# Regrouping the attention slots of a hybrid decoder trunk: scores and products with v in one group, nine projection matmuls on either side of the transposes

## The chip, the cores and the metric

The kernel runs on one core of a Trainium2 chip. Its time is the device time in microseconds of one execution. Three runs of the kernel before took 2824.10, 2826.37 and 2828.47 us; the median, 2826.37 us, is the time before.

The core has engines that run their own instruction lists side by side and meet at semaphores: TensorE (PE in the profile, with its weight loads listed apart as PEld), VectorE (DVE), ScalarE (ACT), GpSimd (POOL) and SyncE (SP), which only issues DMAs here. TensorE reads its operands from SBUF and writes to PSUM, which is used in eight banks of 128 x 512 float32.

## The reference

Two residual layers over 1024 tokens of width 1024, one sequence. Layer 0 mixes tokens by a chunked causal gMLP, layer 1 by causal dilated sliding-window attention; each is followed by a squared-ReLU MLP. Every sub-layer has the form

```python
h = x * (1.0 + scale) + shift            # from a conditioning vector
x = layer_norm(ALPHA * x + gate * f(h), g, b)
```

The change lies in the attention. It has 16 heads of 64 and three patterns, (window, dilation) = (128, 1), (512, 4), (2048, 16), each with its own q, k and v projection of `h` (a weight of 1024 x 9216 in all). For each pattern and head, blocks of 128 queries look at their own block of keys and the one before:

```python
s = einsum('bnqrhe,bnkrhe->bnrhqk', qb, kb) * (E ** -0.5) + bias   # ALiBi
s = where(valid, s, NEG)
m = max(s); p = exp(s - m); l = sum(p)
o = einsum('bnrhqk,bnkrhe->bnqrhe', p / l, vb)
lse = m + log(l)
```

The three patterns' outputs are then added with weights softmax(lse), and the sum is multiplied by an output weight.

## The kernel before, in words

All matmuls take float32 operands that are split into a high and a low part (`split`, L100 to L103: ScalarE casts the high part, VectorE subtracts for the low part), so that one product is three matmuls: high-high, high-low, low-high.

**Tiling of the attention.** Heads go in eight pairs. `order` lists the 24 combinations of pair and pattern, for each pair first dilation 16 (g = 2), then 4 (g = 1), then 1 (g = 0). PSUM's eight banks are shared out at the head of `attention`: two each for scores (`sc`), products with v (`pv`), projections (`mm`) and transposes (`tr`).

**The projections** are a generator, `project()`. A unit is q, k or v of one combination for one half of the tokens; it sums over eight blocks of 128 input features. One step of the generator is one block, three matmuls of 128 x 512 (L1134), and eight steps make a unit. After its last step the unit is taken out of PSUM: v by one ScalarE copy (L1141), q and k by two splits for the two heads (ScalarE and VectorE), q with an additional copy on GpSimd (L1150). When a unit of the second half begins, the weights of a later unit are loaded (SyncE) and split. Seven units are done ahead of the first slot, and from there the projections run ahead of the attention.

**The slots.** `slots` holds 8 x 24 + 8 slots, each with three positions. `attend` puts a combination's work into its eight slots, four for each head of the pair:

- position 0, `scores(m)` (L1191): four matmuls for two query tiles, in every slot; then on VectorE bias, scaling and minimum in one instruction a tile (L1214), and on ScalarE the exponential (L1216). `statistics` of the combination before also stands here, in its first slot.
- position 2, `transposes(m)` (L1236): two to four transposes of probability tiles into one `tr` bank, which ScalarE and VectorE split into `pThi` and `pTlo`. In a combination's first slot `values` (L1176) stands ahead of it, eight transposes of v. `transposes` stand in slots 0 to 3 of a head's four for dilation 4, in 1, 2, 3 and 3 for dilation 1, and in 1 and 3 for dilation 16 (`when`).
- position 1, one slot later, `weighted(m)` (L1249): the products of v with `pThi` and `pTlo`, and behind the last of a head the copy and addition of the two PSUM halves into `oT` (ScalarE L1279, VectorE L1280).

`merge` puts the combination of the three patterns' outputs into the first five slots of the next pair: reading the statistics back from DRAM, the weights (VectorE and ScalarE, L1319), writing and spreading them by DMA, three scalings of 128 x 1024 tiles (one on GpSimd, two on VectorE, L1347) and two additions (L1350). `affine_row` puts work on GpSimd and SyncE into position 1 of the first slots.

**The order.** The main loop (L1415) goes through the slots, and in each through the three positions; behind each position it takes two steps of `project()`, six matmuls:

```python
for pos in slot:
    for f in pos:
        f()
    for _ in range(2):
        if next(stream, True) and n >= last_group:
            ...
            next(fill, None)
```

From slot 183 on the projections are used up; from slot 184 on (`last_group`) the same places are filled with pieces of the output multiplication (`box["begin"]`, psd_wo in the profile), sixteen in all, whose loads are issued in `output()` at the first of them.

The order of this program is a priority, not the last word. A planner goes through it with its own costs and gives each engine its list: an instruction that it believes to be ready goes ahead of an earlier one that it believes is not. Each engine then works through its list strictly in order, and waits where an operand is late. Buffers are given out from pools of fixed size (two `tr` banks, two `pTlo` tiles and so on); an instruction that needs a buffer waits until the one who had it has been read.

Of the kernel before, what the change touches and what calls it, by code (L numbers as in the profile page):

```python
# [35 lines left out]
def trunk(ctx: ExitStack, tc: tile.TileContext, x, c, ada_w, ada_b, ln_g, ln_b, a_w_in, a_b_in,  # L36
# [1010 lines left out]
    def attention(before):  # L1047
# [6 lines left out]
        with ExitStack() as ph:  # L1054
# [345 lines left out]
            def output():  # L1400
                box["oT"] = [act_pair(f"oTs_{half}") for half in range(2)]
                res = Residual(2)
                for i in range(4):
                    res.acc[i] = qk.tile([P, D], F32, name=f"acc_2_{i}", tag=("q0", "q1", "k0", "k1")[i])
                out = box["out"] = OutRows(box["oT"], b_w_out[0], gate, res, prepare, "wo")
                for ch in range(2):
                    out.load(ch)
                    prepare(ch)
                box["begin"] = out.begin()
# [3 lines left out]
                next(stream)  # L1413
            fill = None
            for n, slot in enumerate(slots):  # L1415
                for pos in slot:
                    for f in pos:
                        f()
                    for _ in range(2):
                        if next(stream, True) and n >= last_group:  # L1420
                            if not box:
                                output()
                            fill = box["begin"]
                            next(fill, None)
# [5 lines left out]
    with ExitStack() as ph:  # L1430
        open_psum(ph, "A", tr=3, mm=5)
        done = mixer_a()
    done = mlp(1, done)
    out = attention(done)
    with ExitStack() as ph:
        open_psum(ph, "C", tr=3, mm=5)
# [29 lines left out]
```

## Time and profile before

| | |
|---|---|
| median of three runs | 2826.37 us |
| the profiled execution | 2823.26 us |
| its span, first to last instruction | 2821.5 us |
| mean granted TensorE clock | 0.992 |
| TensorE busy | 2742.5 us, 97% of the span |
| VectorE busy | 1943.7 us, 69% |
| ScalarE busy | 1411.1 us, 50% |
| first scores of the attention | at 1045.3 us |
| last projection matmul in a slot | at 2059.5 us |

A busy TensorE in this profile is one with a matmul under way. A matmul's duration reaches from its start to its modelled end and overlaps that of the next, so what a matmul takes from the engine's time is read from the distance between starts. A number in square brackets in a list by time is idle time of the engine before that instruction, with what ended it. A list of waits names who waited for whom, the total, the number of times and the longest.

### The profile page before, as it was taken

The numbers are of one execution on the slowest core, as the hardware profiler recorded it, in microseconds if no ns is written. First come the engines' busy times: TensorE is split into PE (matmuls) and PEld (weight loads), VectorE is DVE, ScalarE is ACT, GpSimd is POOL, SyncE is SP. The second block draws the span as 40 slices with busy tenths as digits, with TensorE's granted clock in tenths as the row PEclk, the third lists the DMA queues.
The fourth block names the chain that finished last, engine by engine and source line by source line (L and its number), as shares of the span: only waits on it lengthen the run. The fifth ranks groups of instructions, "written<-read, shape, count | busy, mean of one in ns | idle before, by whom it ended". The sixth has DMA issues, their size and how long they took to land.

```text
span 2821.5 us, 36888 instructions
## 1 busy us (share of the span) xinstructions
PE 2742.5 (97%) x13290; PEld 2277.4 (81%) x13290; DVE 1943.7 (69%) x3485; ACT 1411.1 (50%) x2613; POOL 213.9 (8%) x163
## 2 busy tenths in 40 slices
PE   6999999999999999999999999999999999999997
PEld 5777878887888878888888888888877788888886
DVE  6786798777877665556555555555659975577776
ACT  3334275555443455555555555555564755554331
POOL 1021000000000034101000000010201000000000
PEclk9999999999999999999999999999999999999999
DMA  7533347667846443212121212121215564485561
GB/s 254 171 106 112 120 139 232 205 220 256 317 155 194 141 150 106 62 46 61 39 69 39 69 31 69 39 69 39 84 51 175 172 211 151 150 306 190 176 214 58
DMA packets 300186, 384.15 MB, mean 136 GB/s; under 512 B 47532, under 2 KB 172884, under 8 KB 300004
## 3 DMA queue, kind: packets, MB, share of 16 engines
q1 hardware_dynamic: 300004, 381.80, 42.1%
q8 instruction: 104, 1.70, 0.3%
q14 instruction: 78, 0.64, 0.1%
HBM read 297.77 MB, written 83.97 MB: 135 GB/s over the span
## 4 chain that ended last, share of the span: by engine, by line
PE 76%; DVE 11%; DMA 7%; ACT 2%; issue 2%; POOL 1%; SPq 1%; DVEq 0%; POOLq 0%; ACTq 0%
PE psd L938 21%; PE psua L782 9%; PE psq L1134 8%; PE psv L1134 8%; PE psk L1134 7%; PE psuc L782 4%; DMA adaw<-in_ada_w_dram 3%; PE psd_wout L356 3%; PE pv L1262 2%; PE psub L782 2%; PE psu L356 2%; PE psd_wo L356 1%; PE sc L1208 1%; DVE adaacc L128 1%; PE pT L1239 1%
## 5 line engine op out<-in xcount | busy, mean ns | idle before, releaser
L782 PE MATMUL psua<-right,left 128*128 128x512 f32 x1536 | 363.6, 390 | 3.3 <-ACT right L102 1.7
L938 PE MATMUL psd<-rhi,lhi 128*128 128x512 f32 x896 | 350.1, 391 | 2.1 <-ACT part L813 2.1
L938 PE MATMUL psd<-rlo,lhi 128*128 128x512 f32 x896 | 349.6, 390 | 1.4 <-DVE rlo L103 1.3
L938 PE MATMUL psd<-rhi,llo 128*128 128x512 f32 x896 | 349.2, 390 | 0.0
L782 PEld LDWEIGHTS psua<-right,left 128*128 128x128 f32 x1536 | 287.1, 188 | 65.5 <-DVE right L103 3.1
L1216 ACT ACTIVATE p<-p,stat 128x128 f32<-128x128 f32 (+1 forms) x384 | 170.2, 444 | 230.9 <-DVE stat L1214 230.0
L1134 PE MATMUL psv<-hT,wv_hi 128*128 128x512 f32 x768 | 246.8, 403 | 2.4 <-DVE qlo L103 2.4
L1134 PE MATMUL psq<-hT,wq_hi 128*128 128x512 f32 x768 | 248.1, 404 | 0.0
L1134 PE MATMUL psk<-hT,wk_hi 128*128 128x512 f32 x768 | 247.3, 403 | 0.0
L103 DVE TENSOR_TENSOR pTlo<-pT,pThi 128x512 fp32r<-128x512 f32 (+1 forms) x160 | 98.0, 620 | 158.4 <-ACT pThi L102 157.5
L938 PEld LDWEIGHTS psd<-rhi,lhi 128*128 128x128 f32 x896 | 168.5, 188 | 38.3 <-ACT part L813 3.0
L938 PEld LDWEIGHTS psd<-rlo,lhi 128*128 128x128 f32 x896 | 168.6, 188 | 36.7 <-DVE rlo L103 2.4
L938 PEld LDWEIGHTS psd<-rhi,llo 128*128 128x128 f32 x896 | 168.5, 188 | 35.2
L782 PE MATMUL psuc<-right,left 128*128 128x512 f32 x768 | 187.7, 391 | 0.0
L128 DVE SCALAR_TENSOR_TENSOR adaacc<-adaw,silu_c,adaacc 128x512 f32<-128x512 f32 x168 | 130.9, 789 | 67.2 <-DMA adaw<-in_ada_w_dram 66.3
L782 PEld LDWEIGHTS psuc<-right,left 128*128 128x128 f32 x768 | 143.4, 188 | 30.0 <-DVE right L103 0.6
L1280 DVE TENSOR_TENSOR oT<-oT,pv 64x512 f32<-64x512 f32 x96 | 91.0, 948 | 109.5 <-ACT oT L1279 108.8
L1134 PEld LDWEIGHTS psv<-hT,wv_hi 128*128 128x128 f32 x768 | 133.8, 190 | 22.2 <-issue 2.8
L1134 PE MATMUL psq<-hT,wq_lo 128*128 128x512 f32 x384 | 151.4, 394 | 0.0
L1134 PE MATMUL psv<-hT,wv_lo 128*128 128x512 f32 x384 | 151.3, 394 | 0.0
L1134 PE MATMUL psk<-hT,wk_lo 128*128 128x512 f32 x384 | 150.6, 392 | 0.0
L1134 PEld LDWEIGHTS psk<-hT,wk_hi 128*128 128x128 f32 x768 | 133.7, 190 | 19.6
(250 smaller groups left out, 5842.3 us busy)
## 6 DMA issues: line engine op xcount, KB each, us to landing
lraw<-forms SPq DMA_DIRECT2D x112, 512.0 KB, 4.3
adaw<-in_ada_w_dram SPq DMA_DIRECT2D x192, 256.0 KB, 3.0
up<-in_mlp_w_up_dram SPq DMA_DIRECT2D x64, 512.0 KB, 3.8
forms<-s SPq DMA_DIRECT2D x128, 256.0 KB, 2.4
rraw<-in_mlp_w_down_dram SPq DMA_DIRECT2D x64, 512.0 KB, 4.5
forms<-part SPq DMA_DIRECT2D x96, 256.0 KB, 2.5
spill<-acc SPq DMA_DIRECT2D x24, 512.0 KB, 2.6
wq_raw<-in_b_w_qkv_dram SPq DMA_DIRECT2D x24, 512.0 KB, 3.7
```

The source lines that it names most:

```text
L103: return first, lo_engine.tensor_tensor(lo, src, hi, op=ALU.subtract)
L128: ins = V.scalar_tensor_tensor(acc[:], raw[:], silu_c[:, k : k + 1], acc[:], ALU.mult, ALU.add)
L356: T.matmul(dst, s[a], m[b], start=(n == 0), stop=(n == last))
L782: T.matmul(acc, w[:, a, k, :], right[p][:, b, k, :], start=p in (1, 2, 5) and k + a + b == 0, stop=k == 3 and a == 1, skip_group_check=True)
L938: T.matmul(sums[kind, m][:], l[a][:, k, m * P : (m + 1) * P], r[b][:, k, :], start=p in (1, 5, 2, 3) and kp + k + a + b == 0, stop=kp == K ...
L1134: T.matmul(p[:], wu[a][:, k * P : (k + 1) * P], hT[half][b][:, k, :], start=k + c_ == 0, stop=k == KD - 1 and c_ == 2)
L1208: T.matmul(scb[:, sl], my["qlo"][e][:, tq], keys[:, k0 : k0 + w], start=False, stop=True)
L1216: A.activation(pr[:, 0:w], pr[:, 0:w], AF.Exp, bias=nm, scale=-1.0, accum_out=l)
L1239: T.transpose(pst[:, o : o + P], probs[t][:, P : 2 * P] if has[t] else probs[t][:, 0:P], ident[:])
L1262: T.matmul(pvs[b][:, q0 % HALF : q0 % HALF + w_], stt, x_[:, o_ : o_ + w_], start=not begun[b], stop=left[b] == 0, skip_group_check=True)
L1280: V.tensor_tensor(dst, dst, sb, op=ALU.add)
```

## The change

The loop over a slot's three positions becomes a loop over two: positions 0 and 1 are run together, then position 2. Behind each of the two come three steps of the projections (or three pieces of the output multiplication) instead of two behind each of three. A slot still takes six steps.

```diff
             for n, slot in enumerate(slots):
-                for pos in slot:
+                for pos in (slot[0] + slot[1], slot[2]):
                     for f in pos:
                         f()
-                    for _ in range(2):
+                    for _ in range(3):
                         if next(stream, True) and n >= last_group:
                             if not box:
                                 output()
```

So a slot's program order on TensorE changes from scores, six projection matmuls, products with v, six, transposes, six to scores, products with v, nine, transposes, nine.

## The prediction

> **What bounds the kernel now.** I read the page's summary first, then the busy times of the attention stage, then who waits for whom on TensorE in that stage, then single slots in order of time.
>
> ```profile
> span 2821.5 us, 36888 instructions
> PE 2742.5 (97%) x13290; PEld 2277.4 (81%) x13290; DVE 1943.7 (69%) x3485; ACT 1411.1 (50%) x2613; POOL 213.9 (8%) x163
> ```
>
> The stage that the change touches, and what follows it until the last products with v (stretch, length, then busy time and instructions of TensorE, weight loads, VectorE, ScalarE, GpSimd; granted clock, DMA share, GB/s):
>
> ```profile
> 1045.30:2060.00 1014.70, 1011.64 (x5495) 858.87 (x5494) 574.69 (x1393) 557.93 (x1329) 137.54 (x114) 1.00 0.22 60
> 2060.00:2104.00 44.00, 40.94 (x224) 32.80 (x223) 29.21 (x71) 28.03 (x71) 5.20 (x3) 1.00 0.17 50
> ```
>
> TensorE is busy for 1011.64 of 1014.70 us at a granted clock of 1.00, VectorE and ScalarE for 57% and 55%. The stage ends when TensorE has worked off its list; the other engines matter only where a matmul meets an operand that is not ready. The largest of TensorE's waits there (total, times, longest):
>
> ```profile
> PE pT L1239 <- ACT p L1216: 2.3, 4, 1.0
> ```
>
> So 2.3 us in four places, a transpose (pT) waiting for its exponentials (p); the view has one smaller row of the same kind and none for a product with v (pv). One slot in order of time (start, duration):
>
> ```profile
> 1511.25 0.22 PE L1207 MATMUL sc<-k,q 128*128 128x128 f32 x1
> ...
> 1511.60 0.28 PE L1208 MATMUL sc<-k,qlo 128*128 128x256 f32 x1
> 1511.72 0.62 PE L1134 MATMUL psv<-hT,wv_hi 128*128 128x512 f32 x2
> 1512.18 0.40 PE L1134 MATMUL psv<-hT,wv_lo 128*128 128x512 f32 x1
> ...
> 1512.87 0.40 PE L1134 MATMUL psv<-hT,wv_lo 128*128 128x512 f32 x1
> 1513.11 0.28 PE L1262 MATMUL pv<-pThi,v 128*128 128x256 f32 x1
> ...
> 1513.40 0.27 PE L1262 MATMUL pv<-pTlo,v 128*128 128x128 f32 x1
> 1513.51 0.68 PE L1134 MATMUL psv<-hT,wv_hi 128*128 128x512 f32 x2
> ...
> 1514.96 0.27 PE L1239 MATMUL pT<-ident,p 128*128 128x128 f32 x1
> ...
> 1515.20 0.71 PE L1134 MATMUL psv<-hT,wv_hi 128*128 128x512 f32 x2
> ...
> 1516.67 0.22 PE L1207 MATMUL sc<-k,q 128*128 128x128 f32 x1
> ```
>
> Read starts, not durations, since matmuls overlap. Two projections take 1512.18 - 1511.72 = 0.46, so 0.23 each and six 1.38 us. The six take 1.39 behind the scores (1511.72 to 1513.11), 1.45 behind the products (1513.51 to 1514.96) and 1.47 behind the transposes (1515.20 to 1516.67). Scores take 0.47 (1511.25 to 1511.72), products 0.40, transposes 0.24. The slot is 5.42 us and has no hole.
>
> **The change, part by part.** No instruction is added or removed, no DMA either: a slot still has eighteen projections, and the projections last until the same slot. Only the order moves.
>
> *One hand-over less.* The projections behind the scores go; scores run straight into products. The hand-over that is lost is the one that cost 0.01 (1.39 against 1.38); the 0.07 behind the products and the 0.09 behind the transposes stay. Of 24 slots of a head pair 4 + 8 + 6 = 18 (dilations 16, 4, 1) have scores and products both. Seven pairs give 126, less the first slot, plus 10 in the last pair before the projections run out: 135. That is 135 x 0.01 = 1.4 us gained. Scores next to products stand nowhere in the trace while projections run, so this is bounded from the rows above: if what is saved is not the 0.01 but the mean of the three lead-ins, (0.01 + 0.07 + 0.09) / 3 = 0.057, the gain is 7.7 us; if the first product loses its cover and costs the 0.05 by which a 0.11 step (1513.40 to 1513.51) exceeds the 0.06 of a bare 128-column step (128 of a 512-column 0.23), the loss is 6.8 us. I take -1.4, the lead-in that really disappears.
>
> The Trainium skill (TensorE: Matmul & The Clock Gate, Part 3, The mechanism) states that a weight load overlaps running matmuls only when it targets another row group. All loads here are full height, so by that rule no cover exists to be lost or saved, this term would be 0 and the sum 1.4 us higher. The trace disagrees: the load of the first product starts within the projection of 1512.87, at
>
> ```profile
> 1512.88 0.19 PEld L1262 LDWEIGHTS pv<-pThi,v 128*128 128x128 f32 x1
> ```
>
> *Transposes come sooner after their scores.* Between them stood twelve projections and now stand nine: 3 x 0.23 = 0.69 us less for the chain scores, VectorE's minimum, ScalarE's exponential. Matmuls behind a waiting transpose wait too: the nine projections, then the next scores. Where the slack is thin is seen at dilation 16, in the slots where VectorE also scales the last pair's outputs. First the thin places' first and last (TensorE, then ScalarE):
>
> ```profile
> 1064.42 0.60 PE L1239 MATMUL pT<-ident,p 128*128 128x128 f32 x4
> ...
> 2009.77 0.71 PE L1239 MATMUL pT<-ident,p 128*128 128x128 f32 x2 [0.53 <-ACT p L1216]
> ```
> ```profile
> 1063.67 0.39 ACT L1216 ACTIVATE p<-p,stat 128x128 f32<-128x128 f32 x1
> ...
> 2009.62 0.39 ACT L1216 ACTIVATE p<-p,stat 128x128 f32<-128x128 f32 x1
> ```
>
> At 1064.42 the fourth transpose starts some 0.33 later, 0.69 after its exponential ended (1064.06); at 2009.77 it already waits. Of the 32 transpose groups of dilation 16 between these slots and around them, 17 have less than 0.69 us to spare over the closest hand-over that occurs. A typical one of slot 3 of a pair (start of scores and of transposes; exponential; the scaling that holds VectorE):
>
> ```profile
> 1594.89 0.22 PE L1207 MATMUL sc<-k,q 128*128 128x128 f32 x1
> 1598.08 0.62 PE L1239 MATMUL pT<-ident,p 128*128 128x128 f32 x4
> ```
> ```profile
> 1597.83 0.39 ACT L1216 ACTIVATE p<-p,stat 128x128 f32<-128x128 f32 x1
> ```
> ```profile
> 1595.05 1.23 DVE L1347 TENSOR_TENSOR oT<-oT,bc 128x1024 f32<-128x1024 f32 x1
> ```
>
> The exponential ends at 1598.22 and the fourth transpose starts just after; it cannot come 0.69 earlier. Adding up 0.69 less the present spare time over the 17 gives 8.3 us if all of it is exposed, 0 if the planner puts projections ahead. Transposes of dilations 1 and 4 I cost at nothing (a row of theirs stands below). I take half, 4.1 us, because these slots already show waits that the planner did not see: the 0.53 above is one of them.
>
> *Products come sooner after their transposes,* by 0.69 us, and by 2 x 0.69 = 1.38 where the split of the transposed probabilities is held by work that hangs on the slot's start (weight splits, projection evictions). Three places recur in each pair. The tightest, dilation 1, slot 2 (TensorE, ScalarE, VectorE):
>
> ```profile
> 1542.13 0.27 PE L1239 MATMUL pT<-ident,p 128*128 128x128 f32 x1
> ...
> 1543.96 0.28 PE L1207 MATMUL sc<-k,q 128*128 128x256 f32 x1
> ...
> 1545.82 0.29 PE L1262 MATMUL pv<-pThi,v 128*128 128x256 f32 x1
> ```
> ```profile
> 1540.62 0.49 ACT L1216 ACTIVATE p<-p,stat 128x256 f32<-128x256 f32 x1
> ...
> 1543.26 0.59 ACT L102 CAST pThi<-pT 128x512 fp32r<-128x512 f32 x1
> ```
> ```profile
> 1542.66 1.29 DVE L103 TENSOR_TENSOR wk_lo<-wk_raw,wk_hi 128x1024 fp32r<-128x1024 f32 x1 [0.27 <-ACT wk_hi L102]
> 1543.98 0.69 DVE L103 TENSOR_TENSOR qlo<-psq,q 64x512 fp32r<-64x512 f32 x1
> 1544.70 0.69 DVE L103 TENSOR_TENSOR pTlo<-pT,pThi 128x512 fp32r<-128x512 f32 x1
> ```
>
> The low half is ready at 1545.39, 0.43 before the product. VectorE goes through without a break from 1542.66, so it will not be ready sooner, while the product moves up by 1.38: 0.95 late. The transposes of 1542.13 show the cover of their kind: the exponentials that they need had ended by 1540.62, where ScalarE begins a later one, 1.5 us earlier; 0.8 of that is left, and if it went too each such slot would add its shortfall. The two others (product, then its low half):
>
> ```profile
> 1496.84 0.29 PE L1262 MATMUL pv<-pThi,v 128*128 128x256 f32 x1
> ...
> 1529.37 0.28 PE L1262 MATMUL pv<-pThi,v 128*128 128x256 f32 x1
> ```
> ```profile
> 1495.47 0.56 DVE L103 TENSOR_TENSOR pTlo<-pT,pThi 128x384 fp32r<-128x384 f32 x1 [0.56 <-ACT pThi L102]
> ...
> 1528.10 0.56 DVE L103 TENSOR_TENSOR pTlo<-pT,pThi 128x384 fp32r<-128x384 f32 x1
> ```
>
> Spare are 0.81 and 0.71, so late by up to 0.57 and 0.67. Over 7.5 pairs the three are 7.5 x (0.95 + 0.57 + 0.67) = 16.4 us at most, 0 at least. I take a quarter, 4.1 us, because on plain chains the planner has been right (first rival).
>
> *Behind the projections* (2060 to 2104 us) the same sixteen output pieces fill the same slots, three at a time instead of two. The window above has 44.00 - 40.94 = 3.1 us of idle TensorE; that is the bound either way, and I take 0. Weight loads, statistics and the merge's DMAs keep their slot; on SyncE's and GpSimd's queues those of the middle position pass two projection steps, 1.4 us, within slots of 5.4. I take 0, and what would uncover them is a merge whose scaling comes later, which is in the transposes' term.
>
> **Sum.** -1.4 + 4.1 + 4.1 = +6.8 us on the profiled execution's 2823.26, so 2830.1. That execution lies 3.1 us under the median of the runs, 2826.37 (2824.10 to 2828.47), so on their scale 2833.2. I call 0.2%, 5.65 us, about what a measurement can tell from no change; the sum lies just over it.
>
> **The rivals.** *The planner gives the time back (no change).* The order on TensorE is the planner's, which lets projections pass what it believes is not ready. It did so once a pair, where a transpose needs the bank that the transposes of v hold:
>
> ```profile
> 1492.37 1.03 PE L1182 MATMUL psvt<-ident,vT 128*128 128x128 f32 x8
> ...
> 1494.40 0.30 PE L1239 MATMUL pT<-ident,p 128*128 128x128 f32 x1
> ```
> ```profile
> L1239 PEld LDWEIGHTS pT<-ident,p 128*128 128x128 f32 x366 | 49.7, 140 | 16.1 <-ACT p L1216 5.8 <-DVE v L103 1.9
> ```
>
> The transpose stands directly behind those of v in the program, yet five projections came between, and no idle TensorE is recorded there. If it sees every late operand so well, the order before is restored in the thin places and both waiting terms fall to about 1 us each: 2826.4 - 1.4 + 2 = 2827. Against it: the waits of the table above, which it did not foresee. It decides below 5.65 + 1.4 = 7.1 us of exposed waiting. This includes that the change does not do what it says: where products are late, projections again part them from scores.
>
> *Fewer groups are worth more than the scores' lead-in (faster).* If every change of kind on TensorE costs the same and one of three goes, 135 x 0.057 = 7.7 us go with no wait in return: 2818.7. For it: lead-ins of 0.07 and 0.09 exist. Against it: the one that goes is 0.01. It decides once a join saves 5.65 / 135 = 0.042 us.
>
> **How the numbers follow.** Waits partly exposed, slower by over 0.2%: 0.47, the forecast, with a range of its own from 2832 to 2848. Its top is all of both waiting terms: 2826.4 - 1.4 + 8.3 + 16.4 = 2849.7, cut a little because the waits cannot all be missed. Planner restores: 0.36, 2821 to 2832. Faster: 0.17, 2814 to 2821. The range 2820 to 2848 leaves out most of the faster case and the tip of the slower.
>
> **What would show it.** Right: on TensorE in 1045 to 2060 us products (pv) appear as waiting for pTlo, which they do nowhere now, above all in slot 2 of dilation 1; transposes' 2.3 us grow to 5 to 8; the slot of 5.42 us without waits shrinks to 5.41; nine projections behind the transposes take 9 x 0.23 + 0.09 = 2.16. Wrong: no wait on pv and projections standing between scores and products (first rival), or plain slots of 5.38 us and less (second).

## The result, and the profile after

| | before | after |
|---|---|---|
| median of five runs each, side by side | 2826.37 us | 2845.51 us |
| lowest to highest | 2824.10 to 2830.36 | 2842.94 to 2847.96 |
| ratio | | 1.0063, 95% interval 1.0050 to 1.0077 |
| span of the profiled execution | 2821.5 us | 2841.6 us |

The changed kernel is 19.1 us slower by the medians; the ratio with its interval, taken over the runs side by side, is 1.0063. The forecast was 2833.2 us in a range of 2820 to 2848: the sign and the range held, and the loss was nearly three times the 6.8 us of the sum.

The page of after, its span and first part (engine, busy time, share, instructions):

```profile
span 2841.6 us, 36856 instructions
PE 2752.7 (97%) x13290; PEld 2277.9 (80%) x13290; DVE 1944.5 (68%) x3485; ACT 1413.9 (50%) x2613; POOL 220.1 (8%) x163
```

Each engine has as many instructions as before, in 20 us more. TensorE's busy time grew by 10.2 us, that of the others by at most 6.2. The attention stage of after and what follows it until the last products (stretch, length, busy time and instructions of TensorE, weight loads, VectorE, ScalarE, GpSimd; granted clock, DMA share, GB/s):

```profile
1045.30:2079.00 1033.70, 1021.16 (x5498) 857.97 (x5496) 577.02 (x1394) 560.96 (x1330) 138.53 (x114) 1.00 0.21 59
2079.00:2122.00 43.00, 40.18 (x222) 32.50 (x221) 28.53 (x70) 27.74 (x70) 5.58 (x3) 1.00 0.21 50
```

Nearly all of the loss lies in the stage, at the same granted clock of 1.00: idle TensorE grew from 3.1 us to 12.5. The stretch behind it is not longer. Who waits for whom on TensorE in that stage of after (total, times, longest):

```profile
PE pT L1239 <- DVE v L103: 3.6, 8, 0.5
PE pv L1262 <- DVE pTlo L103: 3.5, 9, 0.5
PE pT L1239 <- ACT p L1216: 2.4, 9, 0.6
PE pT L1242 <- ACT p L1216: 1.2, 6, 0.3
```

Together 10.7 us, where before had 3.1 in the same window. The growth is less than the stage lost. One reason is that an idle stretch is counted from the modelled end of the matmul before it. The Trainium skill (Perfetto Trace Analysis, Tensor Engine Instruction (MATMUL, LD_WEIGHTS)) says the same, that the profiler works a matmul's end out and does not observe it; the trace fits that (slot 8 below: 0.43 recorded where the slot grew by 0.61). So I read the loss from starts: from one slot's first scores matmul to the next one's. From the first slot's start to the end of slot 181 the stage takes 1010.75 us before and 1029.00 after. The difference by place in a pair's 24 slots (0 to 7 dilation 16, 8 to 15 dilation 4, 16 to 23 dilation 1), added up over the pairs, here and for the experiments that follow, in us against before:

```
slot of 24                           1     2     3     4     5     7     8     9    10    11    12    13    14    15    18  others   sum
after                              0.9   4.6   1.9  -0.2  -0.5   0.1   5.0  -0.1   3.0  -0.1  -0.5   1.5   1.7  -0.2   1.9    -1.0  18.3
1 copy behind exponentials         1.0   4.6   1.8  -0.3  -0.5   1.8   5.1  -0.1   0.1   1.2  -1.2   1.0  -0.1  -0.1   2.0    -1.1  15.3
2 v split first                    0.9   4.7   1.8  -0.2  -0.5   1.8  -0.1   5.7   2.9  -0.1  -1.2   0.9   1.5  -0.2   2.0    -1.1  18.8
3 k low half on GpSimd             0.5  -0.1   3.2   0.7  -0.5   0.1   5.0  -0.1   0.3  -0.1   5.2   0.7   1.6  -0.2   1.7    -0.8  17.3
4 only dilation 1                 -0.3   0.0  -0.4   0.0  -0.4   0.0   0.0   0.0   0.0   0.0   0.8   0.0   0.0   0.0   1.9    -0.6   0.9
5 scores 9, products+transposes 9  0.0   0.0  -2.1   0.0  15.5   1.9   6.4  -0.7  -0.7   5.0  -1.7  -0.7  -0.6  -0.2  -0.3     0.0  21.7
6 the same, 12 and 6              -0.1   0.0  -3.0  -0.1   7.8   0.7   5.7   0.2  -0.7  -0.7  -0.4  -0.7  -0.6  -0.6  -0.3    -1.7   5.3
7 the same, 15 and 3              -0.3   0.1  -3.3   0.1  27.9  -0.1  -3.5  11.8  -0.7  -0.7  -1.8  -0.7  -0.6  -0.6  -0.4     7.7  34.6
8 the change, 12 and 6            -0.3   4.9  -2.8   2.8  -0.9   0.8  -0.1   2.9  -0.1  -0.1  -1.1   1.3  -0.1   3.3   2.0     0.7  13.0
9 the change but seven slots      -0.1   0.0  -2.1   2.8  -0.1   0.1  -0.1   3.0  -0.1   1.2   1.0   0.0   0.0   3.3  -0.2    -1.1   7.7
10 = 6 from slot 9 on              0.0   0.0   0.2   0.0  -0.6   0.0   0.0  -0.6  -0.7  -0.7  -0.1  -0.7  -0.6  -0.6  -0.3    -1.3  -6.1
11 = 6 and v split first           0.2   0.0  -3.0  -0.1   7.5   0.9  -0.5  -0.6  -0.7  -0.7   1.3   0.1  -0.6  -0.6  -0.3    -1.7   0.9
```

Seven places of each pair (2, 3, 8, 10, 13, 14, 18) carry nearly all of the loss of after; most of the others gain a little. (The column of others hides two larger terms: slots 0 and 6 of row 7 with 3.1 and 6.9, and slot 23 of row 8 with 1.7.) The spans differ by 2 us more; that is mostly what follows the last products, 718.2 us before and 720.3 after, and since it lies between 717.5 and 721.1 over all the profiled runs here, I leave it as scatter.

A slot of dilation 4 without waits (TensorE of after, the same slot as the prediction's; start, duration):

```profile
1520.14 0.22 PE L1207 MATMUL sc<-k,q 128*128 128x128 f32 x1
...
1520.60 0.28 PE L1262 MATMUL pv<-pThi,v 128*128 128x256 f32 x1
...
1521.01 0.67 PE L1134 MATMUL psv<-hT,wv_hi 128*128 128x512 f32 x2
...
1523.13 0.27 PE L1239 MATMUL pT<-ident,p 128*128 128x128 f32 x1
...
1523.38 0.71 PE L1134 MATMUL psv<-hT,wv_hi 128*128 128x512 f32 x2
...
1525.54 0.22 PE L1207 MATMUL sc<-k,q 128*128 128x128 f32 x1
```

Scores 0.46, products 0.41, nine projections 2.12, transposes 0.25, nine projections 2.16: 5.40 where it was 5.42. So the new order itself costs nothing. Three lossy places show what does.

**Slots 10 and 14** (dilation 4, 3.0 and 1.7 us over the pairs). ScalarE in slot 10 of the fifth pair, before:

```profile
1634.51 0.40 ACT L1216 ACTIVATE p<-p,stat 128x128 f32<-128x128 f32 x1 [1.15 <-DVE stat L1214]
...
1634.91 0.49 ACT L1216 ACTIVATE p<-p,stat 128x256 f32<-128x256 f32 x1
...
1635.51 1.07 ACT L1279 COPY oT<-pv 64x512 f32<-64x512 f32 x1
```

And after, ScalarE, the end of the second scaling on VectorE, and TensorE:

```profile
1645.79 0.40 ACT L1216 ACTIVATE p<-p,stat 128x128 f32<-128x128 f32 x1 [1.15 <-DVE stat L1214]
...
1646.19 1.05 ACT L1279 COPY oT<-pv 64x512 f32<-64x512 f32 x1
1647.04 0.49 ACT L1216 ACTIVATE p<-p,stat 128x256 f32<-128x256 f32 x1
```
```profile
1645.96 0.08 DVE L1214 DVE_READ_ACCUMULATOR2_ANT stat<- 128x1 f32 x1
```
```profile
1647.26 0.27 PE L1239 MATMUL pT<-ident,p 128*128 128x128 f32 x1
1647.67 0.33 PE L1242 MATMUL pT<-ident,p 128*128 128x128 f32 x1
```

The products now end 1.4 us sooner in the slot, so the eviction copy of the head is ready sooner, and the planner gave it the place between the two exponentials. The second exponential starts 0.85 behind the copy instead of right behind the first, and the second transpose 0.41 behind the first instead of 0.11. The Trainium skill (PSUM — Partial Sum Buffer, Engine vs sequencer instructions) states that ScalarE's queue is strictly first in, first out; the trace agrees: the exponential's minimum had been read out on VectorE at 1646.04, and it started at 1647.04, behind the copy.

**Slot 2** (dilation 16, 4.6 us). VectorE and TensorE of after:

```profile
1597.37 1.23 DVE L103 TENSOR_TENSOR wk_lo<-wk_raw,wk_hi 128x1024 fp32r<-128x1024 f32 x1 [1.65 <-ACT wk_hi L102]
1598.51 0.68 DVE L103 TENSOR_TENSOR qlo<-psq,q 64x512 fp32r<-64x512 f32 x1
1599.11 0.67 DVE L103 TENSOR_TENSOR pTlo<-pT,pThi 128x512 fp32r<-128x512 f32 x1
```
```profile
1599.22 0.27 PE L1262 MATMUL pv<-pThi,v 128*128 128x128 f32 x1
1599.84 0.33 PE L1262 MATMUL pv<-pTlo,v 128*128 128x128 f32 x1 [0.35 <-DVE pTlo L103]
```

The low half ends at 1599.78 and the second product waits for it: 0.62 between the two starts instead of 0.06 or 0.07. The same place before had its low half at 1590.31, 1.0 us ahead of its use:

```profile
1589.64 0.67 DVE L103 TENSOR_TENSOR pTlo<-pT,pThi 128x512 fp32r<-128x512 f32 x1
```
```profile
1591.31 0.27 PE L1262 MATMUL pv<-pTlo,v 128*128 128x128 f32 x1
```

**Slot 8** (first slot of dilation 4, 5.0 us). VectorE of after splits v here behind the last addition of dilation 16's outputs, and the transposes need the bank that this split frees:

```profile
1635.69 1.08 DVE L1280 TENSOR_TENSOR oT<-oT,pv 64x512 f32<-64x512 f32 x1 [1.37 <-ACT oT L1279]
1636.80 1.29 DVE L103 TENSOR_TENSOR v<-psvt,v 128x512 fp32r<-128x512 f32 x2
```
```profile
1637.54 0.33 PE L1239 MATMUL pT<-ident,p 128*128 128x128 f32 x1 [0.43 <-DVE v L103]
```

They start 6.06 us after the slot's first scores (1631.48). Before it was 6.17 (1620.88 to 1627.05), but with seventeen projections ahead of them. Now there are fourteen, so the transposes could start 0.69 sooner; they start only 0.11 sooner, and the rest comes out as a wait.

### The profile page after: what moved, and what is told of

The parts are those of the page before. It is cut to its first block, busy times and chain, and to the rows that moved or that the text cites. A ratio compares the mean times of both kernels' runs of the same rounds, so it can differ in the third digit from the quotient of the medians.

```text
span 2841.6 us, 36856 instructions
## 1 busy us (share of the span) xinstructions
PE 2752.7 (97%) x13290; PEld 2277.9 (80%) x13290; DVE 1944.5 (68%) x3485; ACT 1413.9 (50%) x2613; POOL 220.1 (8%) x163
## 4 chain that ended last, share of the span: by engine, by line
PE 73%; DVE 11%; DMA 7%; ACT 5%; issue 2%; POOL 2%; SPq 0%; DVEq 0%; ACTq 0%; POOLq 0%
PE psd L938 21%; PE psua L782 10%; PE psv L1134 8%; PE psq L1134 7%; PE psk L1134 5%; PE psuc L782 5%; DMA adaw<-in_ada_w_dram 3%; PE psd_wout L356 3%; PE psub L782 2%; PE pv L1262 2%; PE psd_wo L356 2%; ACT p L1216 1%; DVE adaacc L128 1%; PE psu L356 1%; PE sc L1208 1%
## 5 line engine op out<-in xcount | busy, mean ns | idle before, releaser
L1214 DVE CUSTOM_DVE_ANT_0 p<-sc,bias 128x128 f32<-128x128 f32 (+1 forms) x384 | 119.7, 347 | 68.6 <-PE sc L1208 66.2
L1134 PEld LDWEIGHTS psq<-hT,wq_hi 128*128 128x128 f32 x768 | 135.7, 189 | 22.2
```

What stands on the lines that cost most here:

```text
L1134: T.matmul(p[:], wu[a][:, k * P : (k + 1) * P], hT[half][b][:, k, :], start=k + c_ == 0, stop=k == KD - 1 and c_ == 2)
L1214: V.tensor_tensor_reduce(out=pr[:, 0:w], in0=scb[:, sl], in1=st["bias"][:, width - w :], scale=-0.125, scalar=3e38, op0=ALU.add, op1=ALU.m ...
```

## The experiments

Theory A: the loss is operands that come too late at named places, because the order of ScalarE's and VectorE's lists no longer suits TensorE's. Theory B: scores and products side by side cost in themselves, 135 times a little. Each group of experiments ran beside the kernel before on the same chip; its medians there were 2826.53 (experiments 1 to 4), 2822.10 (5 to 8) and 2827.08 us (9 to 11). The expectations in microseconds count from 2826.5, so for 5 to 8 the ratios are compared. A ratio is taken over the runs and is not the quotient of two medians. All kernels compute the whole of the reference.

**1. The copy behind both exponentials.** The change, with the copy of dilation 4 (one per half of a head, issued where its products end) held in program order on ScalarE.

```diff
-                        if m < len(packs) - 1:
+                        if m < len(packs) - 1 and not (g == 1 and m == 1):
                             return
...
-                        for b in range(2):
+                        for b in range(2) if g != 1 else (m // 2,):
...
-                            A.copy(dst, sa)
+                            ins = A.copy(dst, sa)
+                            if g == 1:
+                                tc.keep_in_program_order(ins)
```

> The changed kernel with one difference: at dilation 4 the copy of the first PSUM half of the products (ScalarE, L1279 of the kernel before) is held behind the slot's second exponential instead of between its two. TensorE's and VectorE's lists stay as in the changed kernel; 16 pairs of ScalarE instructions swap. Theory A (the loss is late operands at named places): the transposes of slots 2 and 6 of dilation 4 no longer wait, which was 3.0 and 1.7 us over the stage against before, so 2845.5 - 4.7 = 2841, slots 106 and 110 back to about 5.41 us. Theory B (the loss is the price of scores and products standing together, 19.1 us over 135 joins): no change, 2845.5.

Measured 2840.9 us, ratio 1.0049 (1.0035 to 1.0062). This interval overlaps with that of the change, 1.0050 to 1.0077, so the time alone says little; the places do. The two exponentials of slot 10 stand together again (ScalarE):

```profile
1646.81 0.40 ACT L1216 ACTIVATE p<-p,stat 128x128 f32<-128x128 f32 x1 [1.15 <-DVE stat L1214]
...
1647.21 0.50 ACT L1216 ACTIVATE p<-p,stat 128x256 f32<-128x256 f32 x1
...
1647.70 1.06 ACT L1281 COPY oT<-pv 64x512 f32<-64x512 f32 x1
```

Slots 10 and 14 gave back all of their 4.7 us. Slot 11 now loses 1.2, and slot 7 of the first pair 1.7 once, so the stage is 2.9 us shorter than in the change, and that the time came out at the expected 2841 is partly chance. The cause of slots 10 and 14 is shown; experiment 3 adds a condition for slot 10.

**2. The split of v first.** The change, with the last copy and addition of dilation 16 issued behind the split of v and held there in program order.

```diff
+            held = []
...
                               pst[:].rearrange("p (t e c) -> p t e c", e=2, c=HEAD))
+                    if held:
+                        held.pop()()
...
+                            if g == 2 and e == 1 and b == 1:
+                                def evict(dst=dst, sa=sa, sb=sb):
+                                    tc.keep_in_program_order(A.copy(dst, sa))
+                                    tc.keep_in_program_order(V.tensor_tensor(dst, dst, sb, op=ALU.add))
+                                held.append(evict)
+                                continue
                             A.copy(dst, sa)
                             V.tensor_tensor(dst, dst, sb, op=ALU.add)
```

> The changed kernel with one difference: in the first slot of dilation 4 the copy and addition of the last products of dilation 16 go behind the split of the transposed v, on ScalarE and on VectorE; TensorE's list stays. Theory A: the transposes there wait for the bank that the split of v frees, and the split stands behind that copy and addition; they come 0.6 us sooner in each of eight pairs, so 2845.5 - 5 = 2840.5, slot 104 from 7.37 to about 6.75 us. Theory B: no change, 2845.5.

Measured 2844.45 us, 1.0064 (1.0051 to 1.0076), the time that theory B expected. By place it is not theory B. Slot 8 gave back its 5.0 us, as expected, and slot 9 took on 5.7. The products there now wait behind the addition; this row was 3.5, 9 in the change:

```profile
PE pv L1266 <- DVE pTlo L103: 6.8, 16, 0.5
```

The cause of the wait in slot 8 is shown, and the time was not gained: it was passed on to the next operand in VectorE's list.

**3. The low half of k's weights on GpSimd.** It takes the 1.23 us ahead of the low half in slot 2 away from VectorE.

```diff
-                    return unit(b_w_qkv[0, :, c0 : c0 + P], f"w{'qkv'[X]}_{hp}_{g}")
+                    return unit(b_w_qkv[0, :, c0 : c0 + P], f"w{'qkv'[X]}_{hp}_{g}", lo_engine=G if X == 1 else V)
```

> The changed kernel with the low half of the k weights made by GpSimd instead of VectorE (24 tiles of 1.23 us). Theory A: in slot 2 of dilation 16 and slot 2 of dilation 1 the products wait for the low half of the probabilities, which stands on VectorE behind that split; these two waits (4.6 and 2.0 us over the stage against before) go, so 2845.5 - 6.5 = 2839. Theory B: no change beyond 1 us.

Measured 2840.39 us, 1.0055 (1.0042 to 1.0068), by the time alone not clear of the change. Slot 2 gave back its 4.6 us. Slot 10 gave back 2.7 of its 3.0, which was not expected: its copy still stands between the two exponentials, but without the split of k's weights on VectorE the first of them starts 1.06 us after the slot's first scores instead of 1.52. So in slot 10 the place of the copy costs time only when the scaling is late as well. Slot 18 kept 1.7 of 1.9, a miss: the planner no longer parted its products with projections. Slot 3 lost 1.3 more, slot 4 0.9, and a single wait of 4.2 us stands in slot 12 of the first pair (ScalarE, then TensorE):

```profile
1120.54 1.04 ACT L102 CAST wv_hi<-wv_raw 128x1024 fp32r<-128x1024 f32 x1 [6.76 <-DMA wv_raw<-in_b_w_qkv_dram]
...
1121.96 0.40 ACT L1216 ACTIVATE p<-p,stat 128x128 f32<-128x128 f32 x1
```
```profile
1122.51 0.33 PE L1239 MATMUL pT<-ident,p 128*128 128x128 f32 x1 [4.23 <-ACT p L1216]
```

Here ScalarE stood idle for 6.76 us ahead of a cast of weights whose load had not landed, and the exponentials stood behind the cast. This slot of the first pair differs from run to run, from 5.3 to 8.4 us in the twelve other profiled runs, but here it takes 11.8. The load was issued 0.9 us after the slot's first scores; in the other runs it was 0.8 to 6.4 us ahead of them. In SyncE's list it stands directly behind the write of an affine row, which waits for GpSimd, and GpSimd now also makes k's low halves, 2.4 us each. So the edit is the likely cause; no run has isolated it.

**4. The change in the slots of dilation 1 alone,** 42 of the 135 hand-overs.

```diff
-                for pos in slot:
+                for pos, steps in (((slot[0] + slot[1], 3), (slot[2], 3)) if n // 8 % 3 == 2
+                                   else ((slot[0], 2), (slot[1], 2), (slot[2], 2))):
...
-                    for _ in range(2):
+                    for _ in range(steps):
```

The last line is the same in experiments 5 to 10, where it is left out; long lines are broken here.

> The kernel before with two groups of nine only in the slots of dilation 1 (42 of the 135 joins). Theory A: these slots account for 1.1 us of the changed kernel's loss, so 2826.4 + 1.1 = 2827.5. Theory B: 42 / 135 of 19.1 us, so 2826.4 + 5.9 = 2832.3.

Measured 2827.11 us, ratio 1.000 (0.999 to 1.001). The stage is 0.9 us longer: 1.9 in slot 18, 0.8 in slot 12, the rest gains. Theory A's 2827.5 fits; theory B's 2832.3, a ratio of 1.0021, lies outside the interval.

**5 to 7. Two groups divided elsewhere:** the scores alone, then products and transposes together, with 9 and 9, 12 and 6, or 15 and 3 projections behind them. One hand-over fewer per slot, as in the change, but scores and products stay apart. The edit of experiment 6 is shown; 5 has 3 and 3 in place of 4 and 2, and 7 has 5 and 1.

```diff
-                for pos in (slot[0] + slot[1], slot[2]):
+                for pos, steps in ((slot[0], 4), (slot[1] + slot[2], 2)):
```

> Two groups again, but divided elsewhere: the scores alone, nine projections, then the products with v and the transposes together, nine projections. Order of TensorE: scores 4, projections 9, products 4, transposes 3, projections 9. One join per slot fewer than before, exactly as in the change, and nine projections in a row, as in the change. The transposes stand 9 projections behind their scores (before 12), as in the change; the products stand 18 behind their transposes instead of 12 (in the change 9). Theory A (late operands: what the change lost came from products too close to their transposes, and from transposes too close to their scores): of the change's 18.2 us by place, slot 2 of dilation 16 (4.6) and slot 18 (2.0) are waits of the products and go; the copies on ScalarE between the two exponentials at slots 10 and 14 (4.7) came from the products ending later in the slot than before, and here they end later still, so these may stay; slot 3 (1.9) and slot 8 (5.0) are waits of transposes and may stay. So 2826.5 plus 5 to 12, about 2834, range 2826 to 2839. Theory B (scores and products with v in one group is what costs): gone, as they are parted: 2826.5, or a little below. Theory C (two groups of nine projections cost as such, whatever stands between them): the change's whole loss again, 2845.

> As the run with the scores alone and nine projections, but twelve projections behind the scores and six behind the products and transposes. Order of TensorE: scores 4, projections 12, products 4, transposes 3, projections 6. The transposes stand 12 projections behind their scores, as before; the products stand 18 behind their transposes (before 12). One join fewer than before, as in the change. Theory A (late operands at named places): no operand comes later than before, so no new wait but those that the later end of the products brings to the copies on ScalarE; 2826.5 less up to 3, that is 2824, range 2821 to 2832. Theory C (two groups cost as such): 2845. Theory of the join (each join that is saved is worth 0.057 us, 135 of them): 2826.5 less 7.7, 2818.8; with 0.01 for each, 2825.

> The scores alone, fifteen projections, products and transposes together, three projections. The transposes stand 15 projections behind their scores (before 12), the products 18 behind their transposes (before 12). Theory A: the transposes' waits that stand in the kernel before (2.3 us and 0.2 us recorded behind the exponentials) go as well, and one join per slot is saved: 2826.5 less 2.5 and less 1.4, about 2822.5, range 2816 to 2832; what can go against it is that three projections behind the transposes hide less of the evictions that free the banks of the next scores and products. Theory C: 2845.

Measured: 2844.44 us, 1.0074 (1.0062 to 1.0086), with 9 and 9; 2829.75, 1.0029 (1.0020 to 1.0039), with 12 and 6; 2861.66, 1.0138 (1.0125 to 1.0151), with 15 and 3. Theory C (two groups of nine cost as such) could live with the first but not with the second. Theory B's 2826.5 failed with 9 and 9, where scores and products stand apart and the loss is as large as the change's. The time that was expected from a join worth 0.057 us, 2818.8, failed too, though experiment 10 will show that these joins save about that much; the waits hid it. Theory A's numbers missed as well, by more than their ranges in all three, and in the last two a gain was expected and a loss came. Of the places it was right about slots 2 and 18, which are free of waits; slots 10 and 14, which it thought might stay, are free too (it had the direction wrong: in the change the products end sooner in the slot, not later). The loss stands in new places, slots 5, 8, 9 and 11. The largest, slot 5 with 12 and 6 (VectorE, then TensorE):

```profile
1609.80 1.05 DVE L1280 TENSOR_TENSOR oT<-oT,pv 64x512 f32<-64x512 f32 x1
1610.76 1.20 DVE L103 TENSOR_TENSOR wv_lo<-wv_raw,wv_hi 128x1024 fp32r<-128x1024 f32 x1
1611.89 1.03 DVE L1280 TENSOR_TENSOR oT<-oT,pv 64x512 f32<-64x512 f32 x1
1612.85 0.27 DVE L1214 CUSTOM_DVE_ANT_0 p<-sc,bias 128x128 f32<-128x128 f32 x1
```
```profile
1613.77 0.71 PE L1239 MATMUL pT<-ident,p 128*128 128x128 f32 x2 [0.46 <-ACT p L1216]
```

The scores of 1609.72 were done by 1610.3; their scaling starts at 1612.85, behind two additions of the head that slot 4 ended and a split of weights between them. In this order the products end some 1.4 us later in the slot, so their eviction falls into the next slot's scaling. I had asked only whether an operand of TensorE comes later in TensorE's own order. What the products release on the other engines moves too, and stands in front of what TensorE needs next. That is theory A with its cause put right after the fact, read from this trace; the next runs rest on it. No run moves the additions of slot 5 alone.

**8. The change's groups with 12 and 6 projections.**

```diff
-                for pos in (slot[0] + slot[1], slot[2]):
+                for pos, steps in ((slot[0] + slot[1], 4), (slot[2], 2)):
```

> The change's own two groups, scores and products together, then transposes, but twelve projections behind the first and six behind the second. Order of TensorE: scores 4, products 4, projections 12, transposes 3, projections 6. The transposes get back their twelve projections behind the scores, the products stand only 6 behind their transposes (before 12, in the change 9). Theory A: the waits of the transposes go (slots 3, 10, 14: 6.6 us; slot 8: up to 5), and the products' waits grow: each place at which they already waited in the change (slot 2 of dilation 16, slot 2 of dilation 1) by three projections of 0.23 us, 0.69 x 8 x 2 = 11 us, and places that had up to 0.7 us to spare join them, unless the planner puts the products later. So 2845.5 less 6.6 to 11.6 and 11 or more added: 2845 to 2860, about 2850, with the waits on the products in the trace and hardly any on the transposes. Theory of the transposes (they alone carry the change's loss): 2845.5 less 12, 2833.

Measured 2838.56 us, 1.0056 (1.0044 to 1.0068). The waits moved as expected: TensorE's largest is on products, and the transposes' waits for exponentials are down to 0.5.

```profile
PE pv L1262 <- DVE pTlo L103: 6.1, 18, 1.0
PE pT L1239 <- ACT p L1216: 0.5, 2, 0.3
```

Slots 3, 8, 10 and 14 are free of loss; slots 4, 9 and 15, whose products now stand six projections behind their transposes, took on 2.8, 2.9 and 3.3. The ratio that was expected, about 2850 / 2826.5 = 1.0083, was missed: slot 2 stayed at 4.9 and slot 18 at 2.0 where I had added 11 for the two. In slot 18 the planner again puts three projections behind the first product. In slot 2 it puts none, but there the low half is ready sooner after its transposes, 2.7 us in most pairs instead of 3.5. The rival's 2833, with the transposes alone, was missed too.

**9. The change without its lossy slots.** Three groups of six in slots 2, 3, 8, 10, 13, 14 and 18, the change's two groups in the other 17.

```diff
-                for pos in (slot[0] + slot[1], slot[2]):
+                for pos, steps in (((slot[0], 2), (slot[1], 2), (slot[2], 2)) if n % 24 in (2, 3, 8, 10, 13, 14, 18)
+                                   else ((slot[0] + slot[1], 3), (slot[2], 3))):
```

> The change's two groups in 17 of the 24 slots of each pair of heads; three groups of six, as before, in the seven at which the change's trace lost its time: slots 2 and 3 of dilation 16 (4.6 and 1.9 us over the pairs), slots 0, 2, 5 and 6 of dilation 4 (5.0, 3.0, 1.6, 1.7) and slot 2 of dilation 1 (2.0). In the orders of ScalarE and VectorE the copies of slots 2 and 6 of dilation 4 stand behind both exponentials again. Theory A (the loss sits at these places): what is left are the 17 other slots, -1.4 us in the change's trace, so 0.9995 of the time before, 0.998 to 1.0015. Theory B (each of the 135 hand-overs from scores to products costs alike): 90 of them stay, 12.2 of the 18.2 us, 1.0043. Theory C (nine projections in a row cost as such): 17/24 of 18.2, 1.0046. Passed on: a place that is healed hands its wait to the next slot with products, as the run with the split of v first did; then also about 1.004, with waits at slots 4, 9, 11 and 15.

Measured 2834.51 us, 1.0034 (1.0021 to 1.0047). Theory A's 0.9995 was missed. By the time alone theory B (1.0043), theory C (1.0046) and the wait that is passed on (about 1.004) all fit. The places tell more. All seven are healed: the sum over them is -2.4 us instead of 19.7, a return of 22.1, where theory B had a third of 18.2 to give back there and theory C 7/24 of it. What is lost is 10.3 us in slots 4, 9, 11 and 15, each the one behind a healed slot, as the last of the expectations had it. But in slots 9 and 15 no wait was handed on, since no operand comes later than before. Slot 9 of the fourth pair (TensorE, then VectorE):

```profile
1497.74 0.30 PE L1239 MATMUL pT<-ident,p 128*128 128x128 f32 x1
...
1498.83 0.39 PE L1262 MATMUL pv<-pThi,v 128*128 128x256 f32 x1
...
1499.42 0.39 PE L1262 MATMUL pv<-pTlo,v 128*128 128x256 f32 x1
```
```profile
1498.81 0.56 DVE L103 TENSOR_TENSOR pTlo<-pT,pThi 128x384 fp32r<-128x384 f32 x1 [0.56 <-ACT pThi L102]
```

The low half is ready 1.63 us after the first transpose (1497.74 to 1499.37). Before it was 1.63 too, by the prediction's rows of the same slot (1494.40 to 1496.03), but the products began 2.44 after that transpose and here begin 1.09 after it. In slot 15 the low half takes 2.86 us both times, and the products begin after 2.18 instead of 3.57. So the mix itself is the cause there: it puts the products of these slots only six projections behind their transposes (six behind the transposes of a slot with three groups, none between scores and products in the next), which I had overlooked. Experiment 8 has that distance everywhere and pays the same in three of these four: in most pairs 0.27, 0.36 and 0.47 us in slots 4, 9 and 15, here 0.27, 0.36 and 0.46. Slot 11 (0.11 a pair here, nothing there) is an exception, and slot 19, at the same distance, loses nothing in either. Whether the change in the harmless slots alone gives 0.9995, as theory A says, was therefore not measured.

**10. The other division, from slot 9 on.** Slots 0 to 8 as before, where the division of experiment 6 lost; scores, twelve projections, products and transposes, six projections in the other 15.

```diff
-                for pos in (slot[0] + slot[1], slot[2]):
+                for pos, steps in (((slot[0], 2), (slot[1], 2), (slot[2], 2)) if n % 24 < 9
+                                   else ((slot[0], 4), (slot[1] + slot[2], 2))):
```

> Three groups of six as before in slots 0 to 8 of each pair's 24; in the other 15 the scores, twelve projections, products and transposes together, six projections. The run that had this order in all slots gained 5.4 us at slots 9 to 23 (0.73 at most of dilation 4's, 0.09 for one slot) and lost 7.8 at slot 5 and 5.7 at slot 8, where the eviction of the products stood ahead of a scaling or of the split of v. Here the orders of VectorE and ScalarE over slots 0 to 9 are those of the kernel before. Theory A: 5.4 us less than before, 0.998 of its time, 0.9965 to 0.9995. The rival (a slot gained at 9 to 23 is given back, since the lists of the other engines end later elsewhere): 1.000.

Measured 2819.83 us, ratio 0.9977 (0.9966 to 0.9987): faster than the kernel before, by the 0.2% that was expected. A slot of dilation 4 (the same as above, TensorE):

```profile
1512.34 0.22 PE L1207 MATMUL sc<-k,q 128*128 128x128 f32 x1
...
1512.80 0.62 PE L1134 MATMUL psv<-hT,wv_hi 128*128 128x512 f32 x2
...
1515.53 0.29 PE L1262 MATMUL pv<-pThi,v 128*128 128x256 f32 x1
...
1515.95 0.29 PE L1239 MATMUL pT<-ident,p 128*128 128x128 f32 x1
...
1516.22 0.71 PE L1134 MATMUL psv<-hT,wv_hi 128*128 128x512 f32 x2
...
1517.67 0.22 PE L1207 MATMUL sc<-k,q 128*128 128x128 f32 x1
```

It takes 5.33 us where before took 5.42: twelve projections in 2.73 (12 x 0.228), products 0.42, transposes 0.27, six in 1.45. The lead-in that is gone is that of the projections behind the products, the 0.07 of the prediction.

**11. Experiment 6 with the split of v first,** the edits of 6 (12 and 6) and 2 together.

> The order with the scores alone, twelve projections, products and transposes together, six projections, in all slots, and the copy and addition of the last products of dilation 16 placed behind the split of v on ScalarE and VectorE. In the change's own order this took 5.1 us from slot 8 and gave 5.8 to slot 9, whose products stood nine projections behind their transposes. Here they stand eighteen behind. Theory A: slot 8 loses its 5.7 us and slot 9 gains at most 0.5; 1.0029 falls to 1.0009 (0.9995 to 1.002). The rival (the 1.05 and 1.08 us of eviction cost TensorE wherever they are put): 1.003, with a wait in slot 9 or 10.

Measured 2828.38 us, 1.0005 (0.9994 to 1.0015), from 1.0029. Slot 8 went from 5.7 to -0.5 and slot 9 from 0.2 to -0.6. The same edit that only passed the wait on in experiment 2 is a gain where the next products stand eighteen projections behind their transposes instead of nine. Slot 5 keeps its 7.5.

## Why the prediction was right, and where it was wrong

Against the 18.3 us of the stage:

| step of the prediction | forecast | trace of after |
|---|---|---|
| one hand-over less | -1.4 | -2.1 (the other slots that gained) |
| transposes of dilation 16 (slots 1, 3 and 5) | +4.1 | +2.3 |
| transposes of dilations 1 and 4 (slots 8, 10, 14) | 0 | +9.7 |
| products (slots 2, 13, 18) | +4.1 | +8.1 |
| others | 0 | +0.3 |

The sign was right and the range held, and the range held partly by luck: its top was made of 16.4 us of products at three named places, of which one lost 1.9, while 9.7 us of transposes and 4.6 of slot 2, which the prediction had at nothing or had not named, filled it instead. Of the signs named in advance, products do wait for their low half (3.5 us), but mainly in slot 2 of dilation 16; the transposes' waits on exponentials are 3.6 us, not 5 to 8.

*One hand-over less* was right: the slot without waits went from 5.42 to 5.39 to 5.41, and nine projections behind the transposes take the 2.16 that was named. The first product's weights load within the scores' last matmul, so no cover was lost (TensorE, then its weight loads):

```profile
1520.48 0.28 PE L1208 MATMUL sc<-k,qlo 128*128 128x256 f32 x1
```
```profile
1520.49 0.19 PEld L1262 LDWEIGHTS pv<-pThi,v 128*128 128x128 f32 x1
```

The sentence of the Trainium skill that the prediction named (TensorE: Matmul & The Clock Gate, Part 3, The mechanism) allows that overlap only for another row group; these two rows again disagree, since both use all 128 rows. Another sentence of the same section also allows a load into a background weight buffer ahead of running matmuls, and the rows do not contradict that one.

*Transposes come sooner after their scores*: the half that I took for dilation 16 was high (4.1 against 2.3). The step that failed is the sentence "Transposes of dilations 1 and 4 I cost at nothing". For dilation 1 it held. For dilation 4 it cost 9.7 us, more than half of the loss. The 1.5 us of spare time that I named as cover were read in a slot of dilation 1 and from a list of ScalarE that the change reorders: with the products 1.4 us sooner, the eviction copy slipped between the exponentials (slots 10 and 14; experiment 1 takes that away and the 4.7 us with it). And in slot 8 I had read the trace wrongly: five projections between the transposes of v and those of p, with no idle time, I took as proof that the planner covers a late operand. What covered it were all seventeen projections of that slot; the five are still there after the change, but three of the others now stand behind the transposes. Experiment 2 takes this wait away too, with nothing gained in the sum.

*Products come sooner after their transposes*: of my three places one was real. Slot 18 (slot 2 of dilation 1) lost 0.27 a pair instead of 0.95, since the planner put three projections between its first product and the rest; the places in slots 1 and 7 of dilation 4 (9 and 15 of the 24) lost nothing, because there the low half does not hang on the slot's start, as the shift of 1.38 supposed. In slot 9 it is ready 1.65 us after the first transpose, as before, so the products came only 0.7 closer, with 0.81 to spare; in slot 15 it is ready after 1.92 instead of 2.86. Slot 13, 0.1 in most pairs and 0.7 in the first, was not named either. Missed was slot 2 of dilation 16, 0.54 in most pairs, 4.6 us in all. It has the row of weight split, low q and low half that I had found in dilation 1: 1.0 spare before, a shift of 1.39 and so 0.4 late by the prediction's own rule, had I applied it to every slot that splits weights. Experiment 3 confirms the cause. No run takes away the waits of slots 3, 13 and 18 alone, so their causes are read from the trace and not tested. That of slot 3 stays open: in experiment 5 its transposes stand nine projections behind their scores as well, and it loses nothing.

*The rivals.* The planner gave time back in one place of seven, about 0.7 us in each pair. That scores next to products are worth more than their lead-in did not show: plain slots of 5.40, not 5.38. But the rival was half right in a way I had not thought of: which of the three lead-ins goes depends on which groups are joined, and joining products and transposes saves 0.09 a slot of dilation 4 and 0.04 a slot of dilation 1.

*Behind the projections* I took 0; from the start of slot 182 to the last products it is 47.28 us before and 46.86 after.

## What to carry to other kernels

A regrouping on a full engine is priced by what the moved matmuls release elsewhere, not only by what they consume: list, for each slot, what VectorE and ScalarE do between the scores and the transposes, and ask whether an eviction that becomes ready sooner, or later, lands in front of a scaling or an exponential. Spare time read from the old trace is cover only while the other engines' lists keep their order, and filler matmuls without idle time hide a late operand rather than show that none is. Measured by place, from starts, a regrouping need not be taken or left as a whole: here joining products and transposes in fifteen of a pair's 24 slots gained 0.2%, while the runs that regrouped all slots went from no clear change (1.0005) to 1.4% slower.

## What the runs showed that I had not expected

The lead-in of a group depends on what stands ahead of it: projections cost about 0.01 us behind scores, 0.05 to 0.07 behind products and 0.08 to 0.09 behind transposes, while transposes take hardly longer behind products (0.27 for three) than behind projections (0.24 to 0.25). And one load that lands late can hold TensorE through ScalarE's list: in experiment 3 the load of wv_raw was issued on SyncE at 1116.03, and the cast that needs it began at 1120.54, 4.5 us later, with the exponentials of that slot behind it. That single wait of 4.2 us is about as large as what the edit gained in slot 2 of eight pairs.
